# Sums of the log decays spread over the partitions by transfers through DRAM instead of by matrix products

## The chip, the core and the metric

The kernel runs on one core of a Trainium2 chip. TensorE (PE) does the matrix products, VectorE (DVE) and ScalarE (ACT) the arithmetic on tiles, GpSimd (POOL) a few small chains, and SyncE (SP) issues the transfers between DRAM and the on-chip memory SBUF. PE writes its results to PSUM. Each engine works through its own list of instructions in a fixed order and waits on semaphores for the others, so an instruction that waits holds up everything behind it in its list. The metric is device time for one execution, in microseconds (us).

## The reference

The model is two layers deep, 256 positions by 1024 features, in float32. Three of its parts are of interest here. The first layer has a hybrid mixer, of which one half is a state space layer in chunks of 128 positions with 16 heads in two groups of 8 (and the other half an mLSTM), and later parts are gated delta layers, of which the program has two, with 16 head-directions each (4 heads, 2 directions, 2 chunks). Both need the same thing: for each head, the matrix of decays between any two positions of a chunk.

```python
a = (dt * A).reshape(b, nc, chunk, G, E)
acs = jnp.cumsum(a, axis=2)
seg = acs[:, :, :, None] - acs[:, :, None, :]
mask = jnp.tril(jnp.ones((chunk, chunk), bool))[:, :, None, None]
Lm = jnp.exp(jnp.where(mask, seg, -jnp.inf))
CB = jnp.einsum('bctgn,bcsgn->bctsg', C, B)
y_diag = jnp.einsum('bctsg,bctsge,bcsgep->bctgep', CB, Lm, xd)
```

So with s on the partitions and t along the free axis, the tile for one head is acs[t] (a row, the same on all 128 partitions) minus acs[s] (a number per partition), capped, and exponentiated. The question of the change is how that row gets onto all 128 partitions.

## The kernel before

Nearly all of PE's work is one kind of product. A weight matrix is fetched in pieces of 1 MB by SP (`fetch`, line 256, into one of 3 buffers named raw), split by ACT into a high part (`hi`, line 201) and by DVE into a low part (`lo`, line 205), each half a piece at a time into one of 4 buffers, and then multiplied in three passes per product (`mm3`, lines 276 to 278), accumulating in PSUM tiles named mm, of which there are 4. Small results of PE go to PSUM tiles named tr, of which there are also 4, and large SBUF tiles of 128x1024 are named g.

The program is written as generators: a chain (here `chain()` of the hybrid part, or the gated delta part) yields between its steps to others (`FILL`, `SIDE`) that bring weight products. The order within each engine's list is then set by a scheduler, which places each instruction by its own estimate of when it becomes ready and what depends on it; instructions of the same chain may be moved ahead of or behind the products around them. A call of `keep_in_program_order` binds one instruction to its written place.

In the hybrid part the steps are these. `narrow` computes the 24 gate columns (line 196). `softplus` (lines 229 to 244) runs on POOL, some 24 small operations one after the other. Line 620 (DVE) multiplies by the coefficients and gives `a`. Lines 622 and 623 (PE) form the running sums `pc`, and line 625 (DVE) copies them to SBUF as `cs`; lines 627 and 628 (ACT) take exponentials of parts of it. `conv` (line 635 on ACT, then three times line 638 on DVE) reads two product tiles mm of one group of weights and writes a tile t; after it the mm tile is free. Lines 661, 727 and 732 (PE) transpose conv's results, and `states` (lines 667 to 675) goes on from them. `decays(g)` (lines 677 to 695) is called once per group: for each of 2 chunks and 8 heads, line 685 multiplies the column of `a` (repeated to 128x128) by a triangular matrix of ones, which leaves the running sum of that head on every partition in PSUM; line 688 (DVE) subtracts `cs` per partition and caps, into a g tile; then line 693 (ACT, exp) and line 694 (DVE) by halves of 128x512. `outputs` (lines 697 on) multiplies by these tiles (lines 700 and 706).

In each gated delta layer lines 1261 to 1264 (PE) form the running sums, line 1266 (DVE) copies them to `gc`, line 1273 multiplies in the same manner for 16 head-directions, line 1277 (DVE) subtracts and caps into the tiles `D`, line 1280 (ACT) takes the exponentials that cross from one chunk to the other straight from PSUM, line 1281 those of `D`. `scores` (lines 1295 to 1303) follows.

## Time and profile before

| what | value |
|---|---|
| time, median of 3 runs | 1720.15 us (1720.03 to 1720.2) |
| the profiled execution | 1719.56 us, its span 1717.8 us, mean PE clock 0.995 |
| PE busy | 1688.1 us, 98% of the span |
| DVE, ACT, POOL busy | 1134.2, 893.8, 326.6 us |
| line 685, 64 records (32 instructions) | 7.8 us |
| line 1273, 64 records (32 instructions) | 7.6 us |
| transfers | 287.65 MB, mean 167 GB/s |

An fp32 product of the form of lines 685 and 1273 leaves two records in the trace. Products overlap in PE's pipeline: a record lasts longer than the distance to the next one, and the distance is what a product costs. In the rows of a timeline stand the start, the duration (of all merged instructions from the first's start to the last's end), the engine, line, operation, the tiles written and read, the count, and in brackets how long the engine had been idle and which instruction released it.

### The profile page before, as it was taken

The page shows a single profiled execution, that of the slowest core. Times are in us where ns is not written, and L with a number is a line of the kernel's source. Part 1 is how long each engine was busy: PE and PEld are TensorE (multiplying, and loading weights), DVE is VectorE, ACT ScalarE, POOL GpSimd, SP SyncE. Part 2 cuts the span into 40 slices and gives each one's busy share as a digit, 9 for nine tenths or more (in the row PEclk, how much of TensorE's full clock was granted, in tenths as well). Part 3 has the DMA queues.
Part 4 walks back from the last instruction along what each step waited for, and adds up shares of the span by engine and source line. Part 5 has one row for each costly group of instructions (what it writes and reads, how often), then busy time and mean ns, then how long its engine had stood idle before and what let it go on. Part 6 is the DMA issues. An engine that isn't in the chain of part 4 may idle for free.

```text
span 1717.8 us, 27101 instructions
## 1 busy us (share of the span) xinstructions
PE 1688.1 (98%) x10518; PEld 1493.1 (87%) x10518; DVE 1134.2 (66%) x2187; ACT 893.8 (52%) x1327; POOL 326.6 (19%) x474
## 2 busy tenths in 40 slices
PE   9999999999999999999899999999999999999998
PEld 8998799788999899987689998788898878889886
DVE  7665578665665466646966664667775766778566
ACT  6444476465444354434465443476446447644643
POOL 2100121001000010002231000244532124364211
PEclk9999999999999999999899999999999999999999
DMA  7555454344655555554224556355444445454442
GB/s 274 185 183 208 138 185 147 126 156 151 211 180 200 178 185 184 194 190 159 90 98 167 179 195 207 145 188 163 153 148 148 169 158 196 148 163 156 149 148 96
DMA packets 63440, 287.65 MB, mean 167 GB/s; under 512 B 23760, under 2 KB 26704, under 8 KB 30288
## 3 DMA queue, kind: packets, MB, share of 16 engines
q1 hardware_dynamic: 63312, 285.92, 48.1%
q8 instruction: 83, 1.36, 0.3%
q14 instruction: 45, 0.37, 0.1%
HBM read 283.28 MB, written 2.62 MB: 166 GB/s over the span
## 4 chain that ended last, share of the span: by engine, by line
PE 83%; POOL 5%; DVE 5%; issue 3%; ACT 2%; DMA 2%; SPq 1%; POOLq 0%; ACTq 0%; DVEq 0%
PE mm L277 25%; PE mm L278 25%; PE mm L276 25%; POOL g L1341 2%; POOL g L1339 2%; DVE lo L205 1%; PE tr L433 1%; DMA g<-dram 1%; ACT hi L201 1%; DVE g L85 1%; POOL lo L205 1%; DVE g L1008 0%; DMA raw<-in_wgu_dram 0%; PE tr L1273 0%; PE tr L1581 0%
## 5 line engine op out<-in xcount | busy, mean ns | idle before, releaser
L205 DVE TENSOR_TENSOR lo<-raw,hi 128x512 fp32r<-128x512 f32 (+1 forms) x1024 | 696.7, 723 | 434.4 <-ACT hi L201 432.9
L201 ACT ACTIVATE hi<-raw 128x1024 fp32r<-128x1024 f32 x530 | 551.0, 1045 | 551.9 <-PE mm L278 245.5
L277 PE MATMUL mm<-g,hi 128*128 128x256 f32 x1760 | 495.8, 282 | 0.0
L276 PE MATMUL mm<-g,hi 128*128 128x256 f32 x1760 | 494.5, 281 | 0.0
L278 PE MATMUL mm<-g,lo 128*128 128x256 f32 x1760 | 493.8, 282 | 0.0
L276 PEld LDWEIGHTS mm<-g,hi 128*128 128x128 f32 x1760 | 331.4, 188 | 1.0 <-issue 0.2
L277 PEld LDWEIGHTS mm<-g,hi 128*128 128x128 f32 x1760 | 331.3, 188 | 0.6
L278 PEld LDWEIGHTS mm<-g,lo 128*128 128x128 f32 x1760 | 330.4, 188 | 0.4 <-issue 0.2
L276 PE MATMUL mm<-hi,g 128*128 128x512 f32 (+1 forms) x800 | 321.0, 402 | 0.7 <-ACT g L201 0.7
L277 PE MATMUL mm<-lo,g 128*128 128x512 f32 (+1 forms) x800 | 319.0, 399 | 1.1 <-DVE lo L205 0.5
L278 PE MATMUL mm<-hi,g 128*128 128x512 f32 (+1 forms) x800 | 317.4, 398 | 0.6 <-DVE g L446 0.2
L277 PEld LDWEIGHTS mm<-lo,g 128*128 128x128 f32 x800 | 151.6, 190 | 37.4 <-DVE lo L205 5.9
L278 PEld LDWEIGHTS mm<-hi,g 128*128 128x128 f32 x800 | 151.1, 189 | 37.7 <-DVE g L205 3.1
L276 PEld LDWEIGHTS mm<-hi,g 128*128 128x128 f32 x800 | 151.3, 189 | 33.5 <-ACT g L201 1.2
L277 PE MATMUL mm<-lo,f 128*128 128x512 f32 x416 | 164.5, 395 | 0.2 <-POOL lo L205 0.2
L278 PE MATMUL mm<-hi,f 128*128 128x512 f32 x416 | 163.9, 396 | 0.0
L276 PE MATMUL mm<-hi,f 128*128 128x512 f32 x416 | 161.6, 398 | 0.0
L212 POOL TENSOR_SCALAR sm<-sm 128x1 f32<-128x1 f32 x18 | 7.8, 432 | 553.0 <-ACT c L70 552.2
L277 PEld LDWEIGHTS mm<-lo,f 128*128 128x128 f32 x416 | 78.1, 188 | 19.4 <-POOL lo L205 0.6
L278 PEld LDWEIGHTS mm<-hi,f 128*128 128x128 f32 x416 | 78.1, 188 | 18.8
L276 PEld LDWEIGHTS mm<-hi,f 128*128 128x128 f32 x416 | 78.1, 188 | 18.1
L90 POOL TENSOR_TENSOR g<-x,g 128x512 f32<-128x512 f32 x12 | 15.4, 1298 | 216.3 <-DVE x L497 170.3
(399 smaller groups left out, 1661.6 us busy)
## 6 DMA issues: line engine op xcount, KB each, us to landing
raw<-in_wgw_dram SPq DMA_DIRECT2D x80, 1024.0 KB, 4.8
raw<-in_wdn_dram SPq DMA_DIRECT2D x44, 1024.0 KB, 4.9
raw<-in_bx_dram SPq DMA_DIRECT2D x24, 1024.0 KB, 4.8
raw<-in_bgate_dram SPq DMA_DIRECT2D x24, 1024.0 KB, 4.8
raw<-in_bw_dram SPq DMA_DIRECT2D x20, 1024.0 KB, 4.8
raw<-in_hyx_dram SPq DMA_DIRECT2D x12, 1024.0 KB, 4.9
raw<-in_bproj_dram SPq DMA_DIRECT2D x12, 1024.0 KB, 4.9
raw<-in_hyw_dram SPq DMA_DIRECT2D x10, 1024.0 KB, 4.9
```

The costliest lines, as they stand in the source:

```text
L85: self.nc.vector.scalar_tensor_tensor(self.src[t][:, s], self.net.x[t][:, s], self.rstd[t], self.gain[:, s], op0=OP.mult, op1=OP.mult)
L90: self.nc.gpsimd.tensor_tensor(self.src[t][:, s], self.net.x[t][:, s], self.gain[:, s], OP.mult)
L201: nc.scalar.activation(hi, src, AF.Copy)
L205: (nc.gpsimd if o and help else nc.vector).tensor_tensor(lo[..., s], src[..., s], hi[..., s].bitcast(F32), OP.subtract)
L212: G.tensor_scalar(r, v, add, EPS, op0=OP.add, op1=OP.add)
L276: mm(out, a[0], b[0], start=start, stop=False)
L277: mm(out, a[0], b[1], start=False, stop=False)
L278: mm(out, a[1], b[0], start=False, stop=stop)
L433: self.nc.tensor.transpose(p[:, k, :], src[:, k * 128:(k + 1) * 128], self.ident)
L1339: G.tensor_tensor(a, Z[:, :m, e:e + 1].to_broadcast([128, m, n]), B[:, e:e + 1, cs].to_broadcast([128, m, n]), OP.mult)
L1341: G.tensor_tensor(Z[:, :m, cs], Z[:, :m, cs], a, OP.add)
```

## The change

The running sums are taken from `cs` (hybrid) and `gc` (delta), which the kernel has anyway with positions on partitions and heads along the free axis. `rows` transposes them on PE (16 rows of 128 positions; twice in the hybrid part for the two chunks, once in each delta layer), ACT copies the result to SBUF, and SP writes it to DRAM, 16 KB in the hybrid part and 8 KB in a delta layer. `spread` reads 8 of those rows, 4 KB, into all 128 partitions of a g tile of 512 KB, with a source that repeats the same 4 KB for each partition: 4 such transfers in the hybrid part (two before the first group of weights, two between the groups' steps), 2 in each delta layer. All are issued by SP, which issues the weights too. The 64 products by triangular matrices (32 in the hybrid part, 16 in each delta layer) are gone. The subtraction and cap read the g tile in SBUF and write it in place. In the delta part the exponentials that cross chunks read that tile before it is overwritten, and the yield to the first side chain stands after the spread now.

```diff
--- before.py
+++ after.py
@@ -147,6 +147,21 @@
     def dram(self, shape):
         self.n += 1
         return self.dp.tile(shape, F32, name=f"dram{self.n}")
+
+    def rows(self, src, n, blocks):
+
+        nc = self.nc
+        p, r = self.pt(), self.t2()
+        for b in range(blocks):
+            nc.tensor.transpose(p[:n, b * 128:(b + 1) * 128], src(b), self.ident)
+        nc.scalar.activation(r[:n, :blocks * 128], p[:n, :blocks * 128], AF.Copy)
+        d = self.dram([blocks, n, 128])
+        nc.sync.dma_start(d.rearrange("b n c -> n b c"), r[:n, :blocks * 128].rearrange("n (b c) -> n b c", b=blocks))
+        return d
+
+    def spread(self, out, d, first, n):
+
+        self.nc.sync.dma_start(out, bass.AP(d.tensor, d.offset + first * 128, [[0, 128], [1, n * 128]]))
 
     def load_const(self, name, cols, parts=128):
         t = self.const(cols, parts=parts)
@@ -599,6 +614,13 @@
                     A.activation(so[t, g], p, AF.Sigmoid)
                 yield
 
+        seg = {}
+
+        def spread_seg(c, g, rows):
+
+            seg[c] = self.g().rearrange("p (e t) -> p e t", e=8)
+            self.spread(seg[c].rearrange("p e t -> p (e t)"), rows, c * 16 + g * 8, 8)
+
         def chain():
 
             fill = iter(FILL)
@@ -626,6 +648,9 @@
             ecs, de = self.small(16), self.small(16)
             A.activation(ecs, cs[:, 1, :16], AF.Exp)
             A.activation(de, pc[:, 64:80], AF.Exp)
+            cs_rows = self.rows(lambda c: cs[:, c, :16], 16, 2)
+            for c in range(2):
+                spread_seg(c, 0, cs_rows)
             dt = sp
 
             cw = self.col("hy_cw").rearrange("p (j k) -> p j k", k=5)
@@ -647,7 +672,7 @@
                     acc = conv(j, ps[i][:, :256])
                     A.activation(bc[:, j], acc.rearrange("p (t c) -> p t c", t=2), AF.Silu)
 
-            xs, xd, st, px, seg, yv = {}, {}, {}, {}, {}, {}
+            xs, xd, st, px, yv = {}, {}, {}, {}, {}
             e8 = lambda z: z.rearrange("p (e q) -> p e q", e=8)
 
             def inputs(g):
@@ -677,16 +702,12 @@
             def decays(g):
 
                 for c in range(2):
-                    seg[c] = self.g().rearrange("p (e t) -> p e t", e=8)
-                    for hb in range(2):
-                        pr = self.pt().rearrange("p (e t) -> p e t", e=4)
-                        for e in range(4):
-                            h = g * 8 + hb * 4 + e
-                            mm(pr[:, e, :], a[:, c, h:h + 1].to_broadcast([128, 128]), self.tri, start=True, stop=True)
-                        for e in range(4):
-                            h = g * 8 + hb * 4 + e
-                            V.scalar_tensor_tensor(seg[c][:, hb * 4 + e, :], pr[:, e, :], cs[:, c, h:h + 1], self.cap,
+                    for e in range(8):
+                        h = g * 8 + e
+                        i = V.scalar_tensor_tensor(seg[c][:, e, :], seg[c][:, e, :], cs[:, c, h:h + 1], self.cap,
                                                    op0=OP.subtract, op1=OP.min)
+                        if c + e == 0:
+                            self.tc.keep_in_program_order(i)
                 for c in range(2):
                     for hb in range(2):
                         half = seg[c][:, hb * 4:hb * 4 + 4]
@@ -737,6 +758,8 @@
             yield next(fill)
             inputs(1)
             outputs(0)
+            for c in range(2):
+                spread_seg(c, 1, cs_rows)
             yield next(fill)
             turn(0)
             states(1)
@@ -1255,7 +1278,6 @@
 
             ss, r, rq, nk = self.small(16), None, self.small(8), self.small(8)
             k = yield from keys(0, ss[:, :8])
-            yield SIDE[0]
 
             pc = self.pt()
             mm(pc[:, 0:8], self.tri, gs[:, 0:8], start=True, stop=True)
@@ -1265,19 +1287,20 @@
             gc = self.small(24)
             V.tensor_copy(gc, pc[:, :24])
             D = [v24(self.g(1024)) for _ in range(2)]
+            gc_rows = self.rows(lambda b: gc[:, :16], 16, 1)
+            for d in range(2):
+                self.spread(D[d].rearrange("p t h c -> p (t h c)"), gc_rows, 8 * d, 8)
+            yield SIDE[0]
             Dc = [v4(self.l2()) for _ in range(2)]
             for d, t in order:
-                pr = v4(self.pt())
                 for h in range(4):
                     c = d * 8 + t * 4 + h
-                    mm(pr[:, h, :], gs[:, c:c + 1].to_broadcast([128, 128]), self.rtri if d else self.tri,
-                       start=True, stop=True)
-                for h in range(4):
-                    c = d * 8 + t * 4 + h
-                    V.scalar_tensor_tensor(D[d][:, t, h, :], pr[:, h, :], gc[:, c:c + 1], self.rcap if d else self.cap,
-                                           op0=OP.subtract, op1=OP.min)
                     if t != d:
-                        A.activation(Dc[d][:, h, :], pr[:, h, :], AF.Exp, bias=gc[:, 16 + d * 4 + h:17 + d * 4 + h])
+                        A.activation(Dc[d][:, h, :], D[d][:, t, h, :], AF.Exp, bias=gc[:, 16 + d * 4 + h:17 + d * 4 + h])
+                    i = V.scalar_tensor_tensor(D[d][:, t, h, :], D[d][:, t, h, :], gc[:, c:c + 1],
+                                               self.rcap if d else self.cap, op0=OP.subtract, op1=OP.min)
+                    if c == 0:
+                        self.tc.keep_in_program_order(i)
                 A.activation(D[d][:, t], D[d][:, t], AF.Exp)
 
             rk = self.small(8)
```

In the changed kernel's own line numbers, line 156 is the transpose in `rows`, 157 ACT's copy, 159 the write to DRAM, 164 the spread, 216 and 220 the splits, 271 the fetch of weights, 291 to 293 the three products, 644 and 645 the running sums, 647 their copy, 660 and 663 the convolution, 686 and 748 transposes, 707 the subtraction and cap, 714 and 715 the exponential and the product behind it.

The change moves instructions. The first place is PE's list in the hybrid part, around the running sums. A name in these lists carries two numbers, and the text uses the last one (mm_2609 for mm_326_2609); mm are product tiles, sm small tiles. Before, the sums stand 116 products behind `narrow`, in the middle of the convolution's fourth group of weights (mm_2609 and 2610), and 44 products before the convolution's first transpose:

```order
L277 MATMUL mm_326_2609<-g_253_2104,hi329_2613 128x256
L278 MATMUL mm_326_2609<-g_252_2103,lo329_2614 128x256
L276 MATMUL mm_326_2609<-g_252_2103,hi329_2613 128x256
L622 MATMUL tr_298_2373<-sm_297_2371,c5_76 128x40
L623 MATMUL tr_298_2373<-sm_297_2371,c6_78 128x16
L277 MATMUL mm_326_2609<-g_253_2104,hi329_2613 128x256
L278 MATMUL mm_326_2609<-g_252_2103,lo329_2614 128x256
```

```order
L292 MATMUL mm_316_2469<-g_255_2106,hi319_2477 128x256
L293 MATMUL mm_316_2469<-g_254_2105,lo319_2478 128x256
L644 MATMUL tr_298_2373<-sm_297_2371,c5_76 128x40
L645 MATMUL tr_298_2373<-sm_297_2371,c6_78 128x16
L156 MATMUL tr_302_2382<-c2_71,sm_299_2376 16x128 x2
L291 MATMUL mm_324_2544<-g_252_2103,hi327_2548 128x256
L292 MATMUL mm_324_2544<-g_253_2104,hi327_2548 128x256
L293 MATMUL mm_324_2544<-g_252_2103,lo327_2549 128x256
```

Now the running sums and the transposes of `rows` stand 64 products behind `narrow`, right behind the second group of weights (mm_2468 and 2469) and ahead of the third (mm_2544 and 2545), 52 products earlier than they did, with 96 products from there to the first transpose of the convolution.

The second place is DVE's list at the same point, where before the convolution (t tiles), the splits of weights (lo) and the copy of the running sums (sm_2376) alternate:

```order
L638 SCALAR_TENSOR_TENSOR t2_315_2519<-mm_310_2457,c21_112,t2_315_2519 128x253
L638 SCALAR_TENSOR_TENSOR t2_316_2525<-mm_311_2458,c21_112,t2_316_2525 128x255
L620 TENSOR_TENSOR sm_297_2371<-sm_294_2339,sm_296_2367 128x40
L638 SCALAR_TENSOR_TENSOR t2_316_2525<-mm_311_2458,c21_112,t2_316_2525 128x254
L638 SCALAR_TENSOR_TENSOR t2_316_2525<-mm_311_2458,c21_112,t2_316_2525 128x253
L205 TENSOR_TENSOR lo353_2762<-raw352_2759,hi353_2761 128x512 x2
L638 SCALAR_TENSOR_TENSOR t2_324_2595<-mm_319_2533,c21_112,t2_324_2595 128x255
L625 COPY sm_299_2376<-tr_298_2373 128x40
L205 TENSOR_TENSOR lo354_2767<-raw352_2759,hi354_2766 128x512
```

```order
L663 SCALAR_TENSOR_TENSOR t2_313_2456<-mm_308_2394,c21_112,t2_313_2456 128x253
L663 SCALAR_TENSOR_TENSOR t2_320_2530<-mm_315_2468,c21_112,t2_320_2530 128x254
L663 SCALAR_TENSOR_TENSOR t2_314_2462<-mm_309_2395,c21_112,t2_314_2462 128x253
L663 SCALAR_TENSOR_TENSOR t2_321_2536<-mm_316_2469,c21_112,t2_321_2536 128x254
L663 SCALAR_TENSOR_TENSOR t2_320_2530<-mm_315_2468,c21_112,t2_320_2530 128x253
L707 SCALAR_TENSOR_TENSOR g_305_2389<-g_305_2389,sm_299_2376,c7_80 128x128 x3
L663 SCALAR_TENSOR_TENSOR t2_321_2536<-mm_316_2469,c21_112,t2_321_2536 128x253
L707 SCALAR_TENSOR_TENSOR g_305_2389<-g_305_2389,sm_299_2376,c7_80 128x128 x4
L707 SCALAR_TENSOR_TENSOR g_306_2391<-g_306_2391,sm_299_2376,c7_80 128x128 x8
L220 TENSOR_TENSOR lo352_2751<-raw351_2748,hi352_2750 128x512 x2
L663 SCALAR_TENSOR_TENSOR t2_329_2606<-mm_324_2544,c21_112,t2_329_2606 128x255
```

Now the convolution's steps of the first two groups all stand behind the copy of the running sums (seven of them end with the third one on mm_2394, which frees that tile for the third group), and 15 of the 16 subtractions on the two spread tiles g_2389 and g_2391 stand ahead of the split lo_2751, the first weights after the convolution's four groups. ACT's list has the same shape: behind the copy of `rows` come four convolution steps, four sigmoid-weighted ones, three exponentials of the spread tiles and then the high part hi_2750.

The third place is DVE's list at the second pair of spread tiles, g_3084 and g_3086, whose transfers stand on SP right behind the fetch of raw_3155; SP has the fetches of raw_2891, 2967, 3090 and 3155 in a row before them, and raw has 3 buffers. Before, no subtraction stands here (they begin 28 rows after the end of this piece):

```order
L205 TENSOR_TENSOR lo376_2981<-raw375_2978,hi376_2980 128x512 x2
L694 TENSOR_TENSOR g_347_2730<-g_347_2730,l2_334_2690 128x512
L205 TENSOR_TENSOR lo377_2986<-raw375_2978,hi377_2985 128x512 x2
L205 TENSOR_TENSOR lo393_3100<-raw392_3097,hi393_3099 128x512 x2
L638 SCALAR_TENSOR_TENSOR t2_371_2962<-mm_366_2900,c21_112,t2_371_2962 128x255
L638 SCALAR_TENSOR_TENSOR t2_371_2962<-mm_366_2900,c21_112,t2_371_2962 128x254
L205 TENSOR_TENSOR lo394_3105<-raw392_3097,hi394_3104 128x512 x2
L638 SCALAR_TENSOR_TENSOR t2_371_2962<-mm_366_2900,c21_112,t2_371_2962 128x253
```

```order
L220 TENSOR_TENSOR lo369_2899<-raw367_2891,hi369_2898 128x512 x2
L715 TENSOR_TENSOR g_305_2389<-g_305_2389,l2_339_2701 128x512
L220 TENSOR_TENSOR lo375_2970<-raw374_2967,hi375_2969 128x512 x2
L220 TENSOR_TENSOR lo376_2975<-raw374_2967,hi376_2974 128x512 x2
L707 SCALAR_TENSOR_TENSOR g_389_3084<-g_389_3084,sm_299_2376,c7_80 128x128 x7
L220 TENSOR_TENSOR lo394_3093<-raw393_3090,hi394_3092 128x512 x2
L707 SCALAR_TENSOR_TENSOR g_390_3086<-g_390_3086,sm_299_2376,c7_80 128x128 x8
L715 TENSOR_TENSOR g_389_3084<-g_389_3084,l2_339_2701 128x512
L663 SCALAR_TENSOR_TENSOR t2_370_2951<-mm_365_2889,c21_112,t2_370_2951 128x255
L220 TENSOR_TENSOR lo395_3098<-raw393_3090,hi395_3097 128x512 x2
```

Now seven subtractions on g_3084 stand behind the split lo_2975, with the next split lo_3093, eight subtractions on g_3086 and the next convolution (t_370, t_371) behind them. PE's transpose of t_370 stands right behind the products of lo_2975, as the transpose of t_371_2962 stood behind those of lo_2986 before.

## The prediction

> **What bounds the kernel now.** The page comes first: the span, the engines' shares and the chain of waits by engine.
>
> ```profile
> span 1717.8 us, 27101 instructions
> PE 1688.1 (98%) x10518; PEld 1493.1 (87%) x10518; DVE 1134.2 (66%) x2187; ACT 893.8 (52%) x1327; POOL 326.6 (19%) x474
> PE 83%; POOL 5%; DVE 5%; issue 3%; ACT 2%; DMA 2%; SPq 1%; POOLq 0%; ACTq 0%; DVEq 0%
> ```
>
> PE is busy for all but 29.7 us of 1717.8. What leaves PE's list is gained, and any new wait of PE is lost, because there is hardly an old wait that could absorb it. The next view is the groups of PE by line, for what leaves and for the kind of transpose that comes.
>
> ```profile
> L685 PE MATMUL tr<-c,sm 128*128 128x128 f32 x64 | 7.8, 275 | 0.0
> L1273 PE MATMUL tr<-c,sm 128*128 128x128 f32 x64 | 7.6, 278 | 0.0
> L752 PE MATMUL tr<-c,sm 128*4 128x128 f32 x2 | 0.5, 272 | 0.0
> ```
>
> The removed products hold PE for 15.4 us, without a wait before them (the last column). The four new transposes cost at most 0.27 each as line 752's, 1.1 together. With every new wait hidden the change is worth 14.3 us. So the question is what the moved order makes PE wait for; PE's timeline and the two chains that feed it answer it.
>
> **The hybrid part, first pair of tiles.** PE before, from the first product behind `narrow` to the first transposes of the convolution; then POOL's softplus, its first and last row, and the DVE operation behind it:
>
> ```profile
> 220.71 0.38 PE L278 MATMUL mm<-g,lo 128*128 128x256 f32 x1
> ...
> 234.56 0.31 PE L622 MATMUL tr<-sm,c 128*128 128x40 f32 x2
> 234.70 0.37 PE L623 MATMUL tr<-sm,c 128*128 128x16 f32 x2
> 240.23 0.38 PE L661 MATMUL tr<-c,t 128*128 128x128 f32 x2
> 240.45 1.06 PE L727 MATMUL tr<-g 128*128 128x128 f32 x8
> ```
>
> ```profile
> 221.17 0.81 POOL L230 TENSOR_SCALAR sm<-sm 128x40 f32<-128x40 f32 x1 [15.31 <-DVE sm L612]
> ...
> 232.83 0.27 POOL L244 TENSOR_TENSOR sm<-sm,sm 128x40 f32<-128x40 f32 x1
> 233.13 0.20 DVE L620 TENSOR_TENSOR sm<-sm,sm 128x40 f32<-128x40 f32 x1 [1.14 <-POOL sm L244]
> 235.75 0.19 DVE L625 COPY sm<-tr 128x40 f32<-128x40 f32 x1
> ```
>
> Before, 116 products from 220.71 to 234.56 cost 0.119 us each, and the running sums find their input ready since 233.33: the softplus chain of 12 us on POOL is covered by products. Now only 64 products cover it. PE arrives at 220.71 + 64 x 0.119 = 228.3 and waits until 233.3, **5.0 us**. The list is fixed, and 96 products that could run stand behind the waiting one.
>
> What follows is a second wait. The third group of weights needs a PSUM tile that the convolution frees, and DVE's convolution now stands behind the copy of the sums, ACT's behind the copy for `rows`. The rows for these (the last is a group of the page, 1045 ns each):
>
> ```profile
> 234.66 0.55 ACT L635 ACTIVATE t<-mm,c 128x256 f32<-128x256 f32 x1
> 237.92 0.22 ACT L627 ACTIVATE sm<-sm 128x16 f32<-128x16 f32 x1
> 242.41 0.39 ACT L734 ACTIVATE l<-tr 128x256 f32<-128x256 f32 x1
> 237.79 1.26 DVE L638 SCALAR_TENSOR_TENSOR t<-mm,c,t 128x255 f32<-128x255 f32 x3
> 239.19 1.29 DVE L205 TENSOR_TENSOR lo<-raw,hi 128x512 fp32r<-128x512 f32 x2
> 256.96 3.19 DVE L688 SCALAR_TENSOR_TENSOR g<-tr,sm,c 128x128 f32<-128x128 f32 x12 [0.33 <-PE tr L685]
> 258.12 0.63 ACT L693 ACTIVATE g<-g 128x512 f32<-128x512 f32 x1 [0.15 <-DVE g L688]
> L201 ACT ACTIVATE hi<-raw 128x1024 fp32r<-128x1024 f32 x530 | 551.0, 1045 | 551.9 <-PE mm L278 245.5
> ```
>
> From 233.3: sums 0.5 (lines 622 and 623), copy 0.2 to 234.0, transposes 0.5 to 234.5, where PE stops. ACT does two exponentials (0.4) and the copy of 16x256 (between 0.22 of line 627 and 0.39 of line 734; I take 0.39, nearest in length) to 234.9, then its first convolution step to 235.4; DVE's steps come 0.40 apart (1.26 for three), and the seventh, which frees the tile, ends at 235.4 + 6 x 0.40 + 0.47 = 238.3. PE waits **3.8 us**. The 96 products end at 238.3 + 11.4 = 249.7, where PE comes to the first transpose of the convolution, against 240.23 before, with the same number of products done: **9.5 us late**. I would give it 8.5 to 11.
>
> The transfers themselves should be hidden here. Their rows (line, size, median time to landing), and what SP waits for:
>
> ```profile
> raw<-in_hyw_dram SPq DMA_DIRECT2D x10, 1024.0 KB, 4.9
> g<-in_gains_dram SPq DMA_DIRECT2D x7, 512.0 KB, 5.8
> dram<-g SPq DMA_DIRECT2D x8, 64.0 KB, 2.4
> g<-in_fgain_dram SPq DMA_DIRECT2D x1, 512.0 KB, 3.2
> SPq L256 <- DVE lo L205: 112.9, 18, 12.8
> ```
>
> The write goes out at 234.9 and lands 2.4 later, 237.3. A spread of 512 KB takes 3.2 to 5.8; the second adds what 512 KB more adds, 4.9 less 3.2, so 1.7. Both are there by 242.2 to 244.8. No row reads one piece of DRAM 128 times, so this bound is the weakest one here. DVE's last eight subtractions (0.26 each: 12 in 3.19) end by 246.9, ACT's last exponential by 247.5, the high part of the next weights behind it (1.06, as line 201) by 248.6 and half its low part (0.69) by 249.3. PE wants it at 251.1, after the transposes of lines 661 and 727 in their new place (1.4 together, line 727's from 240.45 on). Cover is left, 1.8 us; beyond it each us of the spread costs one.
>
> At the old place of the 16 products PE then gains back half of 7.8: the first pair stands at 9.5 - 3.9 = **+5.6 us**.
>
> **The second pair.** Its two spreads stand on SP behind the fetch of raw_3155, which takes the buffer of raw_2891 and so cannot start before lo_2899 is done: the last row above (SP's longest wait 12.8 us) shows that fetches do wait for the splits. The DVE list then has one product with the mask and four half splits, 3.0 us, and then the subtractions that need the spread. The fetch (4.9) and the spread behind it (1.7 more; 3.2 if it only began after the fetch) take 6.6 to 8.1, I take 6.6, since the two rows were used like this above: DVE waits 3.6, with bounds of 5.1 and, if the spread overtakes the fetch, 0. Behind the wait stand 15 subtractions (3.9), four pairs of splits (4.8), three exponentiated halves' products (1.8) and six convolution steps (2.5) up to the last one on t_370: 13.0 us. It ends 16.6 us after lo_2975. Before, the same stretch was this:
>
> ```profile
> 264.71 1.29 DVE L205 TENSOR_TENSOR lo<-raw,hi 128x512 fp32r<-128x512 f32 x2
> 271.74 1.38 DVE L638 SCALAR_TENSOR_TENSOR t<-mm,c,t 128x253 f32<-128x253 f32 x3
> 274.81 0.38 PE L661 MATMUL tr<-c,t 128*128 128x128 f32 x2
> ```
>
> PE came to the transpose 8.8 us after that split's end (266.0 to 274.8), without a wait. If it keeps that distance it now waits 16.6 - 8.8 = **7.8 us**; 4.2 without DVE's wait, 9.3 with 5.1. The other 16 products give back 3.9: +3.9. The hybrid part is at 5.6 + 3.9 = **+9.5 us**.
>
> **The clock.** There is one idle stretch of this size in the trace, and windows of 3.41 us around it show what it leaves behind (time; then PE's busy time first and the granted clock behind POOL):
>
> ```profile
> 839.02 1.12 PE L1060 MATMUL tr<-c,t 128*128 128x128 f32 x4 [5.19 <-POOL t L924]
> 834.70:838.11 3.41, 0.00 (x0) 0.00 (x0) 3.31 (x11) 2.19 (x3) 0.54 (x1) 1.00 0.00 0
> 838.11:841.52 3.41, 2.50 (x11) 2.17 (x11) 3.13 (x14) 1.39 (x3) 3.15 (x6) 0.50 0.00 0
> 844.94:848.35 3.41, 3.41 (x9) 2.21 (x7) 3.24 (x12) 0.00 (x0) 0.73 (x2) 0.50 0.63 202
> ```
>
> After a window without work the clock was 0.50 for three windows, 10.2 us; a window at half speed, full of products, loses 1.7 us. A wait of 7.8 us holds such an empty window wherever the windows lie; one of 5.0 holds one in about half the cases, but the wait of 3.8 right behind it hides most of the loss. So one window to three are lost once, 1.7 to 5.1; I take the middle, **3.4**. The hybrid part: 9.5 + 3.4 = **+12.9**.
>
> The Trainium skill, "TensorE: Matmul & The Clock Gate", Part 1 (the HAM clock gate), says that the array falls to half its clock after an idle window of about 3.4 us and is released after one busy one. The trace agrees on the fall; the release took three windows here, of which only the last was full. By one window alone the cost would be 1.7.
>
> **The gated delta layers.** The order is kinder there. Before:
>
> ```profile
> 1152.81 3.82 PE L1273 MATMUL tr<-c,sm 128*128 128x128 f32 x32
> 1157.88 0.39 PE L276 MATMUL mm<-hi,g 128*128 128x512 f32 x1
> 1158.11 1.03 PE L1295 MATMUL tr<-l 128*128 128x256 f32 x4
> ```
>
> Now 30 products of 512 columns stand between the sums and the new transpose (7.0 us at 0.23, the distance of the last two rows), which covers DVE's copy; 18 more follow before `scores`, so PE is there 11.2 us after the sums. The spread lands 7.0 + 0.3 + 0.4 + 2.4 + 5.8 = 15.9 us after them, some 5 us later than PE's products of `scores`. But these go to PSUM without it, and PE has over 200 products of side chains behind them; DVE waits in its place, ahead of work with that lead. Each layer gains 3.8 less 0.3 = 3.5, **-7.0 for both**. If the lead is too short, the 5 us show on PE and the gain is gone: 0 to -7.0.
>
> **Sum.** +12.9 - 7.0 = +5.9 against the profiled execution of 1719.56, which is 1725.5; the runs' median lies 0.6 above that execution, so **1726 us**. The own range of this forecast, from the bounds above (hybrid 8.5 - 3.9 + 4.2 - 3.9 + 0 at the low end, 11 - 3.9 + 9.3 - 3.9 + 5.1 at the high one, delta -7.0 to 0, not all at one end), is 1718 to 1736.
>
> **Rivals.** *All waits hidden.* PE does not lose what I count, because softplus on POOL ends earlier (its slow rows of 0.8 us are slow beside DVE's splits, and DVE now does other work), or because the products find tiles free. Then 14.3 us are gained: 1705.9. For it speaks that the removed products are certain; against it that the running sums stand 52 products earlier than their input is ready, which would need POOL's 12 us to shrink to 7. Halfway, with the first waits there but the second pair's wait covered, it is 1720.2 + 5.6 - 3.9 - 7.0 = 1715.
>
> *The waits just eat the gain.* Bounds at their low ends: 8.5 - 3.9 + 4.2 - 3.9 = 4.9 for the hybrid part with no loss of clock, -7.0 for delta: 1718, within measurement of no change.
>
> *The spreads are slow.* One piece of 4 KB is read 128 times, and no row shows what that costs. If two spreads move at half the 213 GB/s that a fetch shows (1 MB in 4.9), they take 9.8 us rather than 5 to 7; the first pair then passes its cover of 1.8 by about 2, the second pair's DVE wait grows by 5, and delta loses 2 to 3 of its 7: 1726 + 2 + 5 + 3 = 1736, from the point at which a pair needs over 9 us.
>
> The Trainium skill, "DMA: Bandwidth & Descriptors", "Latency and other measured facts", has transfers whose 128 streams lie at large powers of two apart fall from 207 to 103 GB/s, and infers that they meet in the same memory channel. Streams that start at one address would be the extreme of it; no trace here shows one, and by that rate this rival's price is the one to expect.
>
> **Chances.** The forecast 0.58; waits hidden, fully or halfway, 0.16; eaten gain 0.14; slow spreads 0.12. A difference below 0.2% (3.4 us) cannot be told from none. Faster than that are the hidden case and a part of the eaten one, 0.21; within it the rest of that and the low end of the forecast, 0.16; slower 0.63. The range from 1710 to 1742 leaves out the fully hidden case and the far end of the slow spreads.
>
> **What would show it.** In the profile after: PE idle about 5 us at the running sums (released by DVE's product behind softplus), about 4 before the third group's products (released by the convolution), 7 or so before the transpose of t_370, with clock below 1.0 behind it; DVE waiting for a transfer ahead of its subtractions on g_3084; no PE wait over 1 us beside the delta sums. If the two first waits are missing, the reading of the order is wrong; if they are there and the time is not longer, the price of the second pair or of the clock is.

## The result

| | before | after |
|---|---|---|
| median | 1720.14 us | 1743.57 us (1740.59 to 1744.61, 4 runs) |
| profiled execution, its span | 1719.56, 1717.8 us | 1743.57, 1741.7 us |
| mean PE clock | 0.995 | 0.982 |

The change makes the kernel slower. The ratio is 1.0121, with a 95% interval of 1.0081 to 1.0160; it spans 13.9 to 27.5 us, the medians differ by 23.4, the profiled executions by 24.0. The forecast was +5.9. What follows explains the 24.0 of the two traces. Now and then an execution, of the kernel before too, takes some 20 us longer than the others of its kind; the medians do not show it, the intervals of the ratios do.

The page of the kernel after, the lines that answer to those of before (the span, the engines):

```profile
span 1741.7 us, 26903 instructions
PE 1690.7 (97%) x10394; PEld 1493.6 (86%) x10394; DVE 1134.1 (65%) x2187; ACT 893.2 (51%) x1330; POOL 332.2 (19%) x474
```

PE has 124 records fewer, and yet it is busy 2.6 us longer, and idle for 51.0 us instead of 29.7. So its products became slower and it waits more. POOL is busy 5.6 us longer with the same 474 instructions, which will matter below.

**The hybrid part.** PE's timeline after, at the places that the prediction named (the running sums, the rows' transposes, the third group, the transpose of t_370):

```profile
232.57 0.62 PE L644 MATMUL tr<-sm,c 128*128 128x40 f32 x2 [4.63 <-DVE sm L642]
...
233.87 0.59 PE L156 MATMUL tr<-c,sm 128*16 128x128 f32 x2 [0.29 <-DVE sm L647]
238.38 0.55 PE L291 MATMUL mm<-g,hi 128*128 128x256 f32 x1 [3.92 <-DVE t L663]
...
290.66 0.66 PE L686 MATMUL tr<-c,t 128*128 128x128 f32 x2 [7.84 <-DVE t L663]
```

And windows of 3.41 us of the kernel after (time; PE's busy time and its records; then the granted clock, the share of DMA and GB/s), around the two hybrid waits, around a stretch without any wait, and in the first delta layer:

```profile
228.34:231.75 3.41, 0.00 (x0) 1.00 0.43 94
231.75:235.16 3.41, 1.60 (x6) 0.50 0.65 271
235.16:238.58 3.42, 0.20 (x1) 0.50 0.35 102
238.58:241.99 3.41, 3.41 (x17) 0.50 0.65 210
241.99:245.40 3.41, 3.41 (x31) 1.00 0.00 0
...
282.95:286.36 3.41, 0.00 (x0) 1.00 0.16 22
286.36:289.78 3.42, 0.00 (x0) 0.50 0.69 285
289.78:293.19 3.41, 2.53 (x13) 0.50 0.57 180
293.19:296.60 3.41, 3.41 (x18) 0.50 0.30 127
296.60:300.02 3.42, 3.42 (x15) 0.50 0.02 5
...
351.22:354.63 3.41, 3.41 (x19) 1.00 0.66 271
354.63:358.04 3.41, 3.41 (x10) 0.50 0.00 0
...
1204.55:1207.96 3.41, 1.19 (x10) 1.00 0.67 276
1207.96:1211.37 3.41, 3.13 (x14) 0.50 0.59 214
1211.37:1214.79 3.42, 3.42 (x18) 0.50 0.22 93
1214.79:1218.20 3.41, 3.41 (x18) 0.50 0.46 161
1218.20:1221.61 3.41, 3.41 (x22) 1.00 0.35 147
```

If work in a half-clock window is taken to lose half of its busy time, the hybrid part adds up: waits 4.63 + 0.29 + 3.92 + 7.84 = 16.7; half clock behind the first waits (1.60 + 0.20 + 3.41) / 2 = 2.6, behind the second (2.53 + 3.41 + 3.42) / 2 = 4.7, and in the window from 354.63 another 1.7; the transposes of `rows` 0.6; products gone, -7.8. Together +18.5. It can be checked by counting, in both traces, to the same product on the big weights: the kernel after is 0.6 us ahead at 220 us of the kernel before, 16.7 behind at 310 and 18.2 behind at 350, which is 18.8 for the part. The half is rough: products of 256 columns start 0.213 us apart at half clock (from 238.73 on) and 0.119 apart at full clock, a loss of 0.44, and the window from 354.63 costs 1.5 by the count.

**The delta layers** were to give 7.0 back and cost 6.5 more instead (17.7 us behind at the first layer's start, 24.1 at the end, by the same count). PE's waits, grouped by the waiting line and the releaser (total, times, longest), first a row of before, then two of after:

```profile
PE tr L1368 <- DVE t L1233: 3.9, 4, 1.4
```

```profile
PE mm L291 <- DVE t L1256: 6.1, 2, 3.1
...
PE tr L1391 <- DVE t L1256: 1.6, 2, 1.5
```

A wait of 3 us per layer at the products behind the layer's convolution, each followed by 10.24 us at half clock: the rows from 1207.96 are the first, and they lose 5.0. Waits 6.1, clock 10.0, PE's saving -7.0, and 2.3 less at the transposes of line 1391 (line 1368 before): +6.8 by this sum, 6.5 by the count of products. Some 1.2 us go the other way, at the very start of the trace and between the two parts. Where the wait comes from is seen in the timelines of POOL, DVE, ACT and PE; first of the kernel before, the addition of the two directions' U, DVE's splits near it, and ACT's copy behind the gather from DRAM:

```profile
1171.64 2.39 POOL L1310 TENSOR_TENSOR g<-g,g 128x1024 f32<-128x1024 f32 x1 [15.18 <-DVE g L1299]
1173.26 1.92 DVE L205 TENSOR_TENSOR lo<-raw,hi 128x512 fp32r<-128x512 f32 x2
1182.62 2.13 ACT L1335 ACTIVATE g<-g 64x1024 f32<-64x1024 f32 x1
```

and the same instructions after, with what stands behind ACT's copy:

```profile
1187.81 6.06 POOL L1333 TENSOR_TENSOR g<-g,g 128x1024 f32<-128x1024 f32 x1 [14.38 <-DVE g L1322]
1187.91 3.69 DVE L220 TENSOR_TENSOR lo<-raw,hi 128x512 fp32r<-128x512 f32 x6
1203.13 1.96 ACT L1358 ACTIVATE g<-g 64x1024 f32<-64x1024 f32 x1 [6.73 <-DMA g<-dram]
1205.12 0.47 ACT L1254 ACTIVATE t<-mm,c 128x256 f32<-128x256 f32 x1
...
1205.63 0.48 DVE L1255 SCALAR_TENSOR_TENSOR t<-mm,c,t 128x255 f32<-128x255 f32 x1 [7.90 <-ACT t L1254]
1206.77 0.36 PE L291 MATMUL mm<-g,hi 128*128 128x256 f32 x1 [3.00 <-DVE t L1256]
```

The addition takes 6.06 us instead of 2.39. 3.69 of six splits plus 2.37 is 6.06: it looks as if POOL only began to move data when DVE's six splits were done. Before, ACT's copy starts without a wait; after, ACT stands 6.73 us before it, and with ACT the convolution (line 1254), DVE's share of it and PE. The run e_delta_port tests this reading.

**The transfers** (line of the page: size, median us to landing), then SP's row for the first pair of spreads in the hybrid part, and the two DVE subtractions there that had to wait for a spread:

```profile
g<-dram SPq DMA_DIRECT2D x8, 512.0 KB, 6.7
...
dram<-t SPq DMA_DIRECT2D x2, 8.0 KB, 1.4
dram<-t SPq DMA_DIRECT2D x1, 16.0 KB, 1.4
```

```profile
236.40 0.82 SPq L164 DMA_DIRECT2D g<-dram  x2
...
240.07 0.88 DVE L707 SCALAR_TENSOR_TENSOR g<-g,sm,c 128x128 f32<-128x128 f32 x3 [0.28 <-DMA g<-dram]
...
277.52 1.93 DVE L707 SCALAR_TENSOR_TENSOR g<-g,sm,c 128x128 f32<-128x128 f32 x7 [3.67 <-DMA g<-dram]
```

The median of 6.7 us mixes two cases. The first pair has no fetch right ahead of it, and its two spreads land 3.65 and 4.98 us after their issue, both within 5.4 us. The other six have a fetch of 1 MB within 0.6 us ahead of them and take 6.2 to 8.1.

### The profile page after: what moved, and what is told of

Same layout as the page of the kernel before. It is cut to its first block, busy times and chain, and to the rows that moved or that the text cites. A ratio compares the mean times of both kernels' runs of the same rounds, so it can differ in the third digit from the quotient of the medians.

```text
span 1741.7 us, 26903 instructions
## 1 busy us (share of the span) xinstructions
PE 1690.7 (97%) x10394; PEld 1493.6 (86%) x10394; DVE 1134.1 (65%) x2187; ACT 893.2 (51%) x1330; POOL 332.2 (19%) x474
## 3 DMA queue, kind: packets, MB, share of 16 engines
HBM read 287.47 MB, written 2.65 MB: 167 GB/s over the span
## 4 chain that ended last, share of the span: by engine, by line
PE 77%; DVE 7%; POOL 6%; issue 3%; DMA 3%; ACT 3%; SPq 1%; POOLq 0%; ACTq 0%; DVEq 0%
PE mm L293 23%; PE mm L292 23%; PE mm L291 23%; DMA g<-dram 2%; POOL g L1364 2%; DVE lo L220 2%; POOL g L1362 2%; PE tr L448 1%; ACT hi L216 1%; POOL g L1333 1%; PE tr L721 1%; DVE g L85 1%; POOL lo L220 1%; DVE g L1322 0%; DVE g L1031 0%
## 5 line engine op out<-in xcount | busy, mean ns | idle before, releaser
L291 PEld LDWEIGHTS mm<-g,hi 128*128 128x128 f32 x1760 | 335.0, 190 | 13.0 <-ACT hi L216 7.1
L292 PEld LDWEIGHTS mm<-g,hi 128*128 128x128 f32 x1760 | 335.1, 190 | 1.5 <-issue 1.0
L293 PEld LDWEIGHTS mm<-g,lo 128*128 128x128 f32 x1760 | 334.4, 190 | 0.4 <-issue 0.2
L292 PEld LDWEIGHTS mm<-lo,g 128*128 128x128 f32 x800 | 151.4, 189 | 37.4 <-DVE lo L220 6.2
L90 POOL TENSOR_TENSOR g<-x,g 128x512 f32<-128x512 f32 x12 | 15.4, 1299 | 216.1 <-DVE x L512 170.1
```

Of the source, the lines that this page charges most:

```text
L90: self.nc.gpsimd.tensor_tensor(self.src[t][:, s], self.net.x[t][:, s], self.gain[:, s], OP.mult)
L291: mm(out, a[0], b[0], start=start, stop=False)
L292: mm(out, a[0], b[1], start=False, stop=False)
L293: mm(out, a[1], b[0], start=False, stop=stop)
```

## The experiments

The theory from the two traces: in the hybrid part the time goes to the two places of the forecast (the early sums; the second pair's spreads behind a fetch), each with half clock behind it; in the delta layers a serial chain over DVE, POOL, SP and ACT became longer and sets the end, so that PE's gain turns into a wait. The rivals: slow spreads; idle time alone, with the clock a by-product; and in the delta layers a gain of 7.0 that is only hidden by what the hybrid part left behind. Each run is the change or a part of it with one thing altered; times are against runs of the kernel before on the same chip (medians 1719.3 to 1719.9), with the ratio and its 95% interval.

| run | median, us | against before | ratio |
|---|---|---|---|
| e_hybrid | 1735.57 | +15.8 | 1.0111 [1.0079, 1.0144] |
| e_delta | 1725.83 | +6.0 | 1.0035 [1.0022, 1.0048] |
| e_later_hyb | 1728.73 | +8.9 | 1.0054 [1.0042, 1.0066] |
| e_four_late_hyb | 1721.33 | +1.5 | 1.0003 [0.9984, 1.0021] |
| e_hyb_warm | 1734.81 | +15.4 | 1.0112 [1.0077, 1.0148] |
| e_pair2_hyb | 1717.34 | -2.5 | 0.9989 [0.9963, 1.0015] |
| e_delta_uadd | 1726.98 | +7.2 | 1.0046 [1.0034, 1.0058] |
| e_delta_rows_uadd | 1733.97 | +14.1 | 1.0072 [1.0053, 1.0092] |
| e_delta_gcopy | 1726.84 | +7.3 | 1.0043 [1.0030, 1.0055] |
| e_half_delta | 1719.20 | -0.7 | 0.9982 [0.9956, 1.0008] |
| e_delta_port | 1718.15 | -1.1 | 1.0003 [0.9983, 1.0024] |
| e_combined | 1717.70 | -1.9 | 0.9984 [0.9975, 0.9993] |

### The two halves of the change

The hybrid part alone leaves the delta layers as before; the delta part alone leaves `decays` as before.

```diff
 # e_hybrid, in the gated delta part
-            gc_rows = self.rows(lambda b: gc[:, :16], 16, 1)
-            for d in range(2):
-                self.spread(D[d].rearrange("p t h c -> p (t h c)"), gc_rows, 8 * d, 8)
...
+                    mm(pr[:, h, :], gs[:, c:c + 1].to_broadcast([128, 128]), self.rtri if d else self.tri,
+                       start=True, stop=True)
 # e_delta, in the hybrid part
-            cs_rows = self.rows(lambda c: cs[:, c, :16], 16, 2)
-            for c in range(2):
-                spread_seg(c, 0, cs_rows)
...
+                            mm(pr[:, e, :], a[:, c, h:h + 1].to_broadcast([128, 128]), self.tri, start=True, stop=True)
```

> The change in the hybrid part alone; the delta layers are as before. By the theory of the moved order PE waits 4.6 us at the running sums, 3.9 before the third group of weights and 7.8 before the transpose of t_370, with half the clock for three to four windows behind each of the two stretches, 16.3 of waits and some 8 of clock against 7.8 saved: +17 to +18 us, 1738. Rival: the hybrid part costs only its waits, and what the clock takes is taken back by work that PE would have waited for: +9 to +10, 1730.

> The change in the two delta layers alone. Theory: each layer has a wait of 3.0 us of its own, at the product whose PSUM tile the convolution frees, because ACT stands in a copy that waits for the gather of the added tiles, and the clock falls to half for 10.2 us behind it: +2.5 to +3.5 per layer, +6, 1726. Rival: the wait in the delta layers is a consequence of the hybrid part's lateness or of where the clock's windows happened to lie; alone the change there gains 3.5 per layer: -7, 1713.

The hybrid part alone costs 15.8, by its profile 1733.6 - 1717.8 = 15.8 too: waits of 4.64, 3.92 and 7.21 us and half clock from 231.86 to 242.10 and from 286.47 to 300.12, as in the whole change. The half-clock window from 354.63 of the change (1.5 us) is not there, and the time lies 1.2 below the +17 to +18 expected. The delta part alone costs 6.0 where -7.0 was forecast; PE waits 2.65 and 2.77 us at line 291, and the clock is at half for 10.24 and 3.41 us. So the wait there is the delta part's own, and the rival that made it a consequence of the hybrid part falls. The two halves explain the whole, 15.8 + 6.0 against 23.4, but for 1.6 us, about that one window, and each missed its term of the forecast.

### The hybrid part: the place of the sums

The running sums, rows and first spreads are written behind the convolution of the first two groups of weights, which puts the sums back to PE's old place, 52 products later.

```diff
 # e_later_hyb against e_hybrid: moved from ahead of the first conv loop to behind it
+            pc = self.pt()
+            mm(pc[:, :40], self.tri, a.rearrange("p t c -> p (t c)"), start=True, stop=True)
...
+            cs_rows = self.rows(lambda c: cs[:, c, :16], 16, 2)
+            for c in range(2):
+                spread_seg(c, 0, cs_rows)
```

> The hybrid part alone, with the running sums, their rows and the first two spreads written behind the convolution's first two groups, so that the sums stand on PE where they stood before (116 products behind the gate product); the delta layers are as before. By the theory of the moved order the waits of 4.6 and 3.9 us go, at most 2 to 4 us of waits come at the first pair of tiles since the spreads start 1 us later than the sums did before, and the wait at the second pair stays at 6 to 8 us with its loss of clock: +3 to +8, 1725. Rival: the transfers' latency is what PE pays for, wherever the sums stand; then the first pair waits as long as before, at another place: +15 to +18, 1737.

The two first waits go; one of 1.73 remains, and by the count of products PE is 1.4 us ahead of the kernel before at 270 us. The second pair now waits 8.96:

```profile
PE tr L686 <- DVE t L652: 9.0, 1, 9.0
...
PE tr L686 <- ACT t L649: 1.7, 1, 1.7
```

The time falls by 6.8 from e_hybrid: the first two waits and their clock are worth that. What is left, 8.9, is just above the +3 to +8 expected. It comes from the second pair, but for 1.5: from 346.32 there is a half-clock window behind a full one, as from 354.63 in the change.

### The hybrid part: the second pair's spreads behind a fetch

With the sums where e_later_hyb has them, all four spreads go out together; the second pair no longer stands on SP behind the fetch of raw_3155.

```diff
 # e_four_late_hyb against e_later_hyb
+            for c in (0, 1):
+                spread_seg(c, 1, cs_rows)
...
-            for c in range(2):
-                spread_seg(c, 1, cs_rows)
+            seg.update(seg1)
```

> The hybrid part alone, with the sums at their old place (as in the run before) and all four spreads issued together behind the rows, ahead of the second group's weights; the delta layers are as before. Theory: the wait of 7 to 9 us before the transpose of t_370 comes from the second pair's spreads standing on SP behind a weight fetch that waits for a raw buffer; issued early, that wait and its 13.7 us of half clock go, the 7.8 us of products stay saved, and what is left are waits of 2 to 3 us at the first pair: -4 to +1 us, 1718. Rival: DVE's own order (15 subtractions ahead of splits and convolution) is what makes PE wait, wherever the spreads start: the wait stays at 4 us or more, +4 to +8, 1726.

The wait at the transpose of t_370 is gone, and the time falls by 7.4 to +1.5, just above the range expected; 1.5 of the 7.4 is the half-clock window from 346.32, which this run does not have. What is left are three waits of 1.6 to 1.8 us and one half-clock window; the windows of this run around it:

```profile
260.75:264.16 3.41, 1.54 (x10) 1.00 0.74 281
264.16:267.57 3.41, 3.41 (x18) 0.50 0.28 41
```

So the place of the spreads behind the fetch brought the second wait, as the prediction had it. The run does not separate its two ingredients, though. With the early spreads the scheduler also moved the subtractions: in e_later_hyb DVE waits 4.04 us for the first tile of the second pair and then has 15 subtractions ahead of the convolution, here 15 of the 16 are done by 256.6, ahead of the splits. So how much of the wait is the late transfer, and how much DVE's order (the rival), is left to the prediction's sum, 3.6 and 3.9. And even with both causes gone the 7.8 us of products don't come out. The three waits are at a transpose behind ACT's convolution step (1.72), at a product that reads a low part from DVE (1.64) and at one that reads an ACT result (1.84); whether the four spreads at once are behind the latter two was not separated.

### Is it the idle time or the clock

e_hybrid with 18 products behind `narrow`, where PE waits.

```diff
 # e_hyb_warm against e_hybrid
+            for n in range(18):
+                w = mm(pc[:, 128:256], self.ident, self.tri, start=True, stop=True)
+                if n == 0:
+                    self.tc.keep_in_program_order(w)
             mm(pc[:, :40], self.tri, a.rearrange("p t c -> p (t c)"), start=True, stop=True)
```

> The hybrid part of the change alone, with 18 extra products (128x128, constants only, overwritten later) on PE behind the gate product, 4.3 us of work in front of PE's first wait of 4.6. They compute nothing that is used. Theory of the clock: half speed follows from a window without enough work, not from lateness; with the first wait filled to 0.3 us, no half clock follows there (10.2 us before, of which PE worked 6.7), and though PE has 4.3 us more to do the kernel ends 1 to 3 us sooner than the hybrid part alone: +13 to +16 over the kernel before, 1733. Rival: the clock falls for another reason (the second wait of 3.9 behind it, or the order), so that the extra work is at best hidden: +16 to +20, 1737.

The added 4.3 us of work filled the first wait and cost nothing. The time, +15.4, lies in the theory's range, but by luck: the half clock that was to go did not. The clock still fell, one window later, now from the second wait, which the rival had named (the windows of this run):

```profile
228.58:231.99 3.41, 3.40 (x29) 1.00 0.69 226
231.99:235.40 3.41, 0.78 (x6) 1.00 0.44 118
235.40:238.82 3.42, 1.82 (x8) 0.50 0.84 339
```

Half clock ends at 242.23. So it has two causes in a row there, and removing the first leaves 6.8 of its 10.2 us in place. A window need not be empty: behind one with 0.78 us of work the clock fell. The run does not price the clock apart from the waits (+15.4 for +15.8); what a half-clock window costs without any wait is seen at 354.63 in the change, 1.5 us.

### The hybrid part: only the second pair spread

The first group keeps its products, which need no lead; the second group is spread, issued early, with the sums at their old place. The rows come from PE as products of `a` with the triangle, so they don't wait for DVE's copy.

```diff
 # e_pair2_hyb against e_later_hyb
-            cs_rows = self.rows(lambda c: cs[:, c, :16], 16, 2)
-            for c in range(2):
-                spread_seg(c, 0, cs_rows)
+            cs_rows = self.rows(lambda c: (a[:, c, :16], self.tri), 16, 2)
+            for c in range(2):
+                spread_seg(c, 1, cs_rows)
...
+                if g == 0:   # the products and subtractions of before
```

> The hybrid part alone: the first pair of tiles by products as before, the second pair by spreads issued early; the rows come from PE as products of the a columns with the triangular matrix (16 rows at once), not from a transpose of the copied sums, and the sums stand at their old place. The delta layers are as before. Theory: no wait over 2 us in the hybrid part, half of 7.8 us saved: -2 to -4, 1717. Rival: any transfer among the weights delays DVE's splits and costs as much as it saves: 0 to +3, 1721.

No wait over 0.7 us and no half clock in the hybrid part, as expected; the profile is 2.2 us shorter (1715.6 against 1717.8), the median 2.5. The interval reaches 1.0015, so by itself it cannot be told from no change.

### The delta layers: three attempts at the chain that missed

The addition of U is the POOL instruction whose time changed most (6.06 for 2.39; no other by more than 1 us), and the gather behind it is what ACT waits for. So the addition was put on DVE; then, on top, the rows were made by products; and apart from these the copy behind the gather was put on POOL, so that ACT would not stand before it.

```diff
 # e_delta_uadd against e_delta
-            G.tensor_tensor(U[0], U[0], U[1], OP.add)
+            V.tensor_tensor(U[0], U[0], U[1], OP.add)
 # e_delta_rows_uadd against e_delta_uadd
-            gc_rows = self.rows(lambda b: gc[:, :16], 16, 1)
+            gc_rows = self.rows(lambda b: (gs[:, b * 8:b * 8 + 8], self.rtri if b else self.tri), 8, 2)
 # e_delta_gcopy against e_delta
-            A.activation(B[lower].rearrange("p j i -> p i j"), turn[lower], AF.Copy)
+            G.tensor_copy(B[lower].rearrange("p j i -> p i j"), turn[lower])
```

> The delta layers alone, with the addition of the two halves of the tiles U on DVE instead of POOL, where it took 6.06 us after the change and 2.39 before. Theory: that addition on POOL, slowed beside DVE's splits, is what makes the gather late by about the length of PE's wait; on DVE (some 1.2 us, behind four half splits) the tiles are ready 2 to 3 us earlier, the wait of 3.0 falls below 1 and the clock stays up: -5 to -7, 1714. Rival: the spreads make the tiles D late, and the addition has nothing to do with it: wait and clock loss stay, +4 to +6, 1725.

> The delta layers alone, both directions by spreads, the rows by products on PE (ready some 7 us sooner than by the transpose of the copied sums) and the addition of the two halves of U on DVE. Theory: with spread and addition both sooner the chain to the gather is no later than before, no wait over 2 us stays in the delta layers: -3 to -6, 1715. Rival: what costs is the order that DVE and ACT get when subtractions, splits and convolution no longer wait for PE's products; waits of 2 to 4 us come at another link: +2 to +7, 1724.

> The change in the delta layers alone, with the copy of the gathered tiles (64x1024) on POOL, which needs them next, instead of on ACT; the hybrid part is as before. Theory: PE's wait of 2.7 us exists because ACT stands in that copy for 6.4 us with a convolution step behind it; with the copy on POOL that wait and the half clock behind it go. The chain over POOL still ends about 3 us later than before, so a wait of 1 to 3 us stays at the convolutions behind it: -3 to +1 us, 1718.5. Rival: the chain over POOL alone sets the end of the layer, whatever stands behind the copy on ACT: +4 to +7, 1725.

All three lost against e_delta, and their theories' ranges were missed. On DVE the addition takes 1.22 us and the wait at line 291 goes, but new ones come 40 us later (the waits of e_delta_uadd, then of e_delta_gcopy):

```profile
PE tr L1390 <- DVE t L1255: 7.5, 2, 3.8
```

```profile
PE tr L1390 <- DVE t L1255: 14.0, 2, 7.0
```

Measured from a layer's first product to the end of POOL's solve, the chain takes 113.5 and 113.8 us in the kernel before, 116.5 and 116.8 in e_delta, 118.8 and 118.9 in e_delta_uadd, 120.8 twice in e_delta_gcopy: in both of the latter the solve itself, some 34 us before, takes 37.4 and 37.9. Moving an operation to another engine changed the order around it, and in these two the wait moved with the end of the chain rather than going. (The traced execution of e_delta_uadd, 1731.49 us, is the slowest of its five: 6.4 us of it are lost around 840 to 870 us, ahead of the delta layers, with a second half-clock stretch there; the waits above are those of the delta layers.) In e_delta_rows_uadd the write of U met a fetch that had gone out a little earlier (SP, then ACT):

```profile
1170.90 0.33 SPq L271 DMA_DIRECT2D raw<-in_bw_dram  x1
1172.01 0.38 SPq L1351 DMA_DIRECT2D dram<-g  x1
...
1178.55 3.90 SPq L1355 DMA_DIRECT2D g<-dram  x4
...
1183.84 2.10 ACT L1357 ACTIVATE g<-g 64x1024 f32<-64x1024 f32 x1 [7.15 <-DMA g<-dram]
```

From write to gather it is 6.5 us there, 3.5 in the change. So an earlier addition gained nothing at ACT. And the chain takes 115.9 and 115.5 us there, less than in e_delta, while the two layers take 8.1 and 7.0 us longer than before, for 3.0 and 2.8 in e_delta. A second link did that: before and in e_delta ACT does two steps of the convolution ahead of its copy of line 1384 (now 1406), here they stand behind it while it waits for another gather (ACT in e_delta_rows_uadd), and PE waits 5.9 us at the transposes that need them:

```profile
1226.41 0.42 ACT L1406 ACTIVATE g<-g 128x256 f32<-128x256 f32 x1 [4.52 <-DMA g<-dram]
...
1227.68 0.46 ACT L1253 ACTIVATE t<-mm,c 128x256 f32<-128x256 f32 x1
```

So the length of the chain goes with the time in e_delta_uadd and e_delta_gcopy, but does not set it alone: what ACT has queued behind a copy that waits counts as well, as the rival of that run had it. The theory that the engine of the addition is the remedy fell.

### The delta layers: one direction spread

One direction keeps its products, the other is spread, with rows by products.

```diff
 # e_half_delta against e_delta
+            gc_rows = self.rows(lambda b: (gs[:, 8:16], self.rtri), 8, 1)
+            self.spread(D[1].rearrange("p t h c -> p (t h c)"), gc_rows, 0, 8)
...
+                if d == 1:
+                    src = D[d][:, t]
+                else:   # the products of before, into src
```

> The delta layers alone, one direction of the tiles D by products as before, the other by a spread whose rows come from PE as products (8 rows at once), issued before the copy of the sums is done. The hybrid part is as before. Theory: the chain from U to the gather is late only because the first subtractions wait for the spread; here they start as before, so the wait of 3.0 us does not come and half of 7.6 us is saved: -2 to -4, 1717. Rival: it is the addition on POOL (6.06 us beside DVE's splits) that makes the gather late; it stays slow here: wait and clock loss stay, 0 to +4, 1722.

The addition takes 2.37 us again, ACT's wait for the gather is 0.78, and the waits at line 291 are gone; in the second layer one of 3.14 is left, with one half-clock window. -0.7 us, less than the -2 to -4 expected: the loss is gone, and nearly all of the gain too. The run does not tell its theory (late subtractions) from its rival (the slow addition), since both are gone in it.

### The delta layers: the cause by itself

The addition and the six splits begin 0.1 us apart in the change. Here one DVE operation of 0.26 us per layer is moved behind the last one that the addition needs. DVE's list is otherwise the same, PE's but for a few products that change places with near neighbours, and ACT, POOL and SP have the same lists.

```diff
 # e_delta_port against e_delta, in scores, for the last head of U
-                            if t == d:
+                            if t == d and (h < 3 or dst_c is not Uc):
...
+                    for t in range(2 if h == 3 and dst_c is Uc else 0):
+                        V.scalar_tensor_tensor(dst_c[t][:, h, :], Dc[t][:, h, :], scal[:, t * 12 + h:t * 12 + h + 1],
+                                               p[:, t, (1 - t) * 128:(2 - t) * 128], op0=OP.mult, op1=OP.mult)
```

> Delta part alone, as in the run of that part, with one DVE operation per layer moved: the product of 128x128 that belongs to the crossing decays of the last head (0.26 us) now stands behind the last product that the addition of U needs, together with the other one of its kind. So the addition on POOL is released about 0.5 us before DVE's six low splits begin, where it was released 0.1 us before them. Theory (the addition cannot run beside those splits: 6.06 us is 3.69 of splits plus 2.37 of its own; and it is the first link of the chain addition, write, gather, copy, solve, that sets the end of each layer): the addition takes 2.4 us in both layers, the six splits take 5 to 6 us instead of 3.7, ACT's wait for the gather falls from 6.4 to some 3 us, PE's waits of 2.7 us before the products that follow the convolution and the half clock behind them go, the chain from a layer's first product to the end of the solve is 113 us instead of 116.5, and the time is 1717 to 1720, 6 us or more below the delta part alone (1725.8). Rival one (the splits come later and PE waits for them instead): the addition takes 2.4 but a wait of 2 us or so appears at a product that reads a low part, with half clock behind it, and the time stays at 1723 or more. Rival two (the addition is slow for another reason, such as the transfers or where its tiles lie): it takes 6 us again and the time is 1726.

All its numbers came (POOL, DVE, ACT in this run):

```profile
1169.35 2.38 POOL L1335 TENSOR_TENSOR g<-g,g 128x1024 f32<-128x1024 f32 x1 [14.10 <-DVE g L1321]
...
1169.71 5.59 DVE L220 TENSOR_TENSOR lo<-raw,hi 128x512 fp32r<-128x512 f32 x6
...
1181.20 2.10 ACT L1360 ACTIVATE g<-g 64x1024 f32<-64x1024 f32 x1 [2.77 <-DMA g<-dram]
```

Now DVE's splits stand back, 5.59 us for 3.69, and the addition takes 2.38. ACT waits 2.77 instead of 6.4, the chain takes 112.5 and 113.3 us, PE's longest wait at line 291 is 0.7, and one half-clock window of 3.41 us is left in the delta layers, in the second. The median is 7.7 us below that of e_delta, 7.1 if each is taken against the kernel before on its own chip. Against the kernel before the interval is wide and holds 1; the medians are 1718.15 and 1719.28. Of the rivals' signs none is there: PE's waits at products that read a low part stay at 0.5 us, and the addition is fast. So the addition's turn behind the splits is shown to be the cause of the delta loss. The 7.0 of the forecast still don't appear: with the chain no shorter than before by more than 0.5 to 1.0 us a layer, there is that much to gain, and the time fell by 1.1.

### Both halves in their best form

e_combined is e_pair2_hyb and e_half_delta together.

> The second pair of the hybrid part by early spreads and one direction of the delta layers by a spread, both as in the runs before, together. Theory: the parts lie 800 us apart and add up, -2.0 and -0.7 us by medians: -2 to -4, 1717. Rival: the delta part's gain was within the scatter of its runs: -1 to -2, 1718.5.

1717.70 us, a ratio of 0.9984 with an interval below 1: 0.16% less than before, and 1.5% less than the change. It takes away 32 of the 64 products, by the rows of before 7.7 us of PE's list, of which 1.9 reach the time; waits of 6.9 us in all are left at the transposes of the delta layers. In its trace the hybrid part is 2.2 us ahead of the kernel before, and 1.5 of that is lost again from 334.66 on, in a half-clock window behind a full one, as in the change. The delta part of e_delta_port in its place was not tried.

## Why the prediction missed by 18 us

**The order and the waits of the hybrid part: right.** PE idle at the sums 4.6 + 0.3 (5.0 forecast), before the third group 3.9 (3.8), before t_370 7.8 (7.8), released as named; the first spread just in time, DVE 0.28 us short of it; DVE's wait at the second pair 3.67 (3.6). e_later_hyb and e_four_late_hyb confirm the two places one after the other; at the second, the late transfer and DVE's order were not separated.

**The clock: one term, mis-sized.** The forecast took "one window to three", 3.4, and argued that "the wait of 3.8 right behind it hides most of the loss". Measured: 2.6 + 4.7 + 1.7 = 9.0. The clock fell at the first pair too, since the two waits together left an empty window and two nearly empty ones, and PE was back at full load for 3.4 us before the release; behind the second wait it was released after four windows, not three. This is 5.6 of the 18 us, and all that the hybrid part missed by the sum, +18.5 for +12.9 (the waits were 16.7 for 16.6). 1.7 of the 9.0 is the window from 354.63, whose cause is open and which e_hybrid does not have.

**The delta layers: the wrong sign.** The step that failed is "DVE waits in its place, ahead of work with that lead". Beside the delta sums there was no wait of PE, as forecast; the wait came 46 us behind them. The lead of PE over DVE was counted; what DVE's new order does to the other engines was not. DVE does not even wait for the spread in these layers: ACT does, 2.0 us in each, and DVE's subtractions stand behind splits by then. The harm comes later in DVE's list, where six splits now stand together behind the products that follow the subtractions: they begin 0.1 us after POOL's addition, where before the first split came 1.6 us after it (1173.26 to 1171.64). That costs 3.7 us on the way to the gather, and PE, which runs some 3.5 us ahead by then, finds the convolution late. The term of -7.0 was +6.5. The bound named for a lead too short, 0, was also wrong, because the wait brings its half clock: 10.0 us in the two layers.

**The transfers: a row for each now.** The small writes land in 1.4 us, below the 2.4 taken. The first spread of the first pair lands in 3.65, within the 3.2 to 5.8 taken; those behind a fetch take 6.2 to 8.1, above it. In the hybrid part the first pair came just in time, DVE 0.28 us short of it.

**The rivals.** The hidden waits and the eaten gain fall with the waits themselves. The slow spreads fall by their own condition: no pair takes over 9 us (5.4 for the first), and DVE has the second pair's first tile 7.2 us after SP begins to issue it (270.37 to 277.52) and comes to the second without a wait. No run here shows the halved rate that "DMA: Bandwidth & Descriptors" of the Trainium skill led one to expect for that rival. The first pair moved its 1 MB in 5.4 us, where a fetch of 1 MB takes 4.9. That the time came out above the range is due to losses that no rival held: the addition's turn behind the splits, and half clock behind waits that look short.

## What to carry to other kernels

Work taken from the busiest engine is worth only what the next chain allows: follow the serial chain that ends the stage, over all engines, and ask for its slack before booking the gain. Price a wait of PE with the clock behind it: here each wait of 3 us in the delta layers cost about 8, an estimate from 3.05 of wait and 5.0 of half clock. And a transfer that replaces a product wants its place on the queue ahead of the next large fetch, and its result before the engine that uses it has other work queued behind.
